# Feed-forward stages of a decoder trunk: six seven-product pairs per duo, and a running sum that ScalarE copies into the PSUM banks

## Chip, cores and metric

The kernel runs on one core of a Trainium2 chip. The metric is the time of one execution in microseconds (us), measured on the device; the kernel before took 2179.21 us (median of 3 runs, 2178.29 to 2180.29). One execution was also recorded by the hardware profiler; the profile and the trace are of that one.

## What is computed

A trunk of two layers on 256 tokens of width 2048, in float32: a gated linear attention mixer, a feed-forward layer, a differential attention mixer, a feed-forward layer. The change is in the two feed-forward layers:

```python
D_MODEL, SEQ, D_FF = 2048, 256, 5632

def swiglu(h, w_gate_up, w_down):
    gate, up = jnp.split(h @ w_gate_up, 2, axis=-1)
    return (jax.nn.silu(gate) * up) @ w_down

f = swiglu(rmsnorm(x, pre_ffn_g[i]), ffn_w_gate_up[i], ffn_w_down[i])
x = x + rmsnorm(f, post_ffn_g[i])
```

## The kernel before

**Matmuls in three products.** TensorE is given operands in a rounded float32 form. Each float32 operand is split in a high part (`hi`, the rounded value) and a low part (`lo`, what rounding left), and a product of two operands is three matmuls: high by high, high by low, low by high. `triple` (L438) issues these three for one stationary block of 128 tokens and 512 columns of weights; `mm_act` (L361) does so twice, for the two row blocks that one weight unit holds.

**Weights.** A weight unit is 128 x 1024 numbers, 512 KB. `weight_stream` lists all units in the order of use, `load` (L256) fetches them on SP's queue into five raw buffers, and `convert` splits them: ScalarE casts the high part (L294) and VectorE subtracts to get the low part (L296). `take` (L349) hands out the next unit and lets `pump` convert further ones; nine pairs of `hi` and `lo` buffers bound how far conversion may run ahead, and the five raw buffers how far loads may.

**Duos and pairs.** A gate chunk and an up chunk of 512 columns are computed together as a "duo" (`duo_apart`, L485), over eight pairs of row blocks. A plain pair takes 8 triples, 24 matmuls, and two weight units. A fast pair uses seven products in place of eight (a 2 x 2 block scheme): 7 triples, 21 matmuls. For that VectorE adds the two raw units in four ways (`sums`, L310, the adds at L317, 128 x 512 each), and four operands `a`, `b`, `c`, `d` are split, three of 128 x 1024 and one of 128 x 512 (`d`). The tokens' side of the seven products is formed once per stage by `build_forms` (L538). `FAST_FFN` names the fast pairs of the duos of chunks 2 to 10 (five pairs: 0, 2, 3, 4, 6), `FAST_SECOND` those of chunk 1 (four). Chunk 0 is computed without fast pairs.

**Banks.** PSUM has eight banks; six have the tag `acc`, two the tag `tp`. A duo uses all: products 0 to 5 in `acc`, product 6 and the last plain sum in `tp`. After the last fast pair, `early` (in `gated_duo`, L1120) takes products 0, 4, 5 and 6 out of their banks (a copy by ScalarE, L1137, and four VectorE operations, L1126); in the last plain pair `late` adds the remaining banks (L1126), ScalarE applies the SiLU (L1148) and VectorE multiplies gate by up (L1130). `gate_T` transposes the gated chunk on TensorE (`split_T`, L602) and splits it.

**The down product.** Its rows are taken in groups of one or two chunks (`FF_GROUPS`), each group in two halves of two output chunks (the group of one in a single call). `down_act` (L413) takes two banks per output chunk, one per 128 tokens, sums the products of the group there, and calls `evac`: the first group's sum is copied to the float32 tile `f` by ScalarE (L1200); every later group's is added to `f` by VectorE (L1202). With the last group `evac` also squares the sum (L630, ScalarE) and multiplies it by the gain (L1206, VectorE), and `add_norm` (L677) normalises and adds to `x`.

**Order.** `ffn_steps` alternates duos and down halves: duo, half, duo, half, with two duos and two halves per group of two chunks. The code is written in program order with small deferred steps (`defer`, `tick`); a scheduler then sets each engine's order from a simulated timeline and priorities. Each engine executes its queue in order.

## Time and profile before

| | |
|---|---|
| time, median of 3 runs | 2179.21 us |
| span of the profiled execution | 2177.2 us |
| time outside the span, against the median | 2.0 us |
| TensorE matmuls busy | 2162.6 us, 99% |
| TensorE weight loads busy | 1798.1 us, 83% |
| VectorE busy | 1932.7 us, 89% |
| ScalarE busy | 1267.2 us, 58% |
| granted TensorE clock, mean | 0.999 |
| first feed-forward stage | about 385 to 1062 us |
| second feed-forward stage | about 1500 to 2168 us |

The profiled execution has no separate time of its own outside the trace: its span stands for it, and 2.0 us are counted as lying around it. In the rows of a view, the first number of a timeline or chain row is the start in us from the span's start, the second the duration in us; a bracket tells how long the engine sat idle before the row and what ended that. In a row of groups the count stands behind x, then busy us and mean ns of one, then the idle time before them. In a row of waits stand the total, the times and the longest, in us. In a row of windows stand, after the length, busy us and instructions of TensorE, of its weight loads, of VectorE, ScalarE and GpSimd, then the granted clock, the DMA share and GB/s.

### The profile page before, as it was taken

Reading aid. Unit: us, or ns where it says so; the run is one execution under the profiler, and the core shown is the slowest. Engines: PE = TensorE matmul, PEld = TensorE weight load, DVE = VectorE, ACT = ScalarE, POOL = GpSimd, SP = SyncE. Lnnn points to the kernel's source line nnn. Section 1 sums busy time; section 2 is a strip of 40 time slices with the busy share of each in tenths; the row PEclk is TensorE's granted clock in tenths of the full one; section 3 lists DMA queues with packets and bytes.
Section 4 is the critical chain, followed back from the end, with each engine's and each line's share of the span. In section 5 each row is a group of like instructions: output and inputs, shape, how many; then the busy total and the mean of one; then the engine's idle time right before and its main releaser. Section 6 shows DMA issues by size and latency. Waiting matters only on the chain.

```text
span 2177.2 us, 28399 instructions
## 1 busy us (share of the span) xinstructions
PE 2162.6 (99%) x10098; PEld 1798.1 (83%) x10098; DVE 1932.7 (89%) x2646; ACT 1267.2 (58%) x1744; POOL 35.6 (2%) x66
## 2 busy tenths in 40 slices
PE   9999999999999999999999999999999999999998
PEld 8887788888888888888878888888888888888886
DVE  7989988998999999998898567889999999999986
ACT  8656665665655555554676455556566555555553
POOL 1000000000000000000000000000000000000000
PEclk9999999999999999999999999999999999999999
DMA  8545566666655566665757655465656555666664
GB/s 309 169 149 191 177 228 213 213 221 215 228 176 199 194 213 213 194 224 189 243 187 248 186 174 161 151 235 189 231 194 223 182 185 195 209 206 212 212 213 135
DMA packets 123315, 440.09 MB, mean 202 GB/s; under 512 B 13899, under 2 KB 16628, under 8 KB 121380
## 3 DMA queue, kind: packets, MB, share of 16 engines
q1 hardware_dynamic: 121996, 436.44, 60.2%
q10 hardware_dynamic: 1176, 1.84, 0.3%
q8 instruction: 79, 1.29, 0.2%
q14 instruction: 64, 0.52, 0.1%
HBM read 429.82 MB, written 9.97 MB: 202 GB/s over the span
## 4 chain that ended last, share of the span: by engine, by line
PE 96%; DVE 2%; DMA 1%; issue 1%; ACT 1%; POOL 0%; SPq 0%; DVEq 0%; POOLq 0%; ACTq 0%
PE acc L444 13%; PE acc L443 13%; PE acc L442 13%; PE acc L372 10%; PE acc L370 10%; PE acc L371 10%; PE acc L585 8%; PE acc L586 4%; PE tp L443 3%; PE tp L444 3%; PE tp L442 3%; PE tp L606 1%; DVE lo L296 1%; PE acc L1307 0%; PE acc L1346 0%
## 5 line engine op out<-in xcount | busy, mean ns | idle before, releaser
L294 ACT CAST hi<-raw 128x1024 fp32r<-128x1024 f32 x905 | 929.5, 1051 | 656.6 <-DVE raw L317 272.7
L296 DVE TENSOR_TENSOR lo<-raw,hi 128x1024 fp32r<-128x1024 f32 x903 | 1077.6, 1220 | 151.8 <-ACT hi L294 148.9
L370 PE MATMUL acc<-hi,f_ffn_gT 128*128 128x512 f32 x704 | 274.1, 390 | 0.0
L371 PE MATMUL acc<-lo,f_ffn_gT 128*128 128x512 f32 x704 | 274.0, 390 | 0.0
L372 PE MATMUL acc<-hi,f_ffn_gT 128*128 128x512 f32 x704 | 268.9, 389 | 0.0
L444 PE MATMUL acc<-hi,h_ffn 128*128 128x512 f32 x666 | 259.6, 390 | 0.0
L443 PE MATMUL acc<-lo,h_ffn 128*128 128x512 f32 x666 | 259.2, 389 | 0.0
L442 PE MATMUL acc<-hi,h_ffn 128*128 128x512 f32 x666 | 258.4, 390 | 0.0
L372 PEld LDWEIGHTS acc<-hi,f_ffn_gT 128*128 128x128 f32 x704 | 132.2, 188 | 27.3
L370 PEld LDWEIGHTS acc<-hi,f_ffn_gT 128*128 128x128 f32 x704 | 132.2, 188 | 27.2
L371 PEld LDWEIGHTS acc<-lo,f_ffn_gT 128*128 128x128 f32 x704 | 132.2, 188 | 27.0
L444 PEld LDWEIGHTS acc<-hi,h_ffn 128*128 128x128 f32 x666 | 125.0, 188 | 26.5 <-issue 0.6
L443 PEld LDWEIGHTS acc<-lo,h_ffn 128*128 128x128 f32 x666 | 125.1, 188 | 25.9
L442 PEld LDWEIGHTS acc<-hi,h_ffn 128*128 128x128 f32 x666 | 125.0, 188 | 25.9
L585 PE MATMUL acc<-h_q,hi 128*128 128x512 f32 x256 | 92.5, 401 | 0.0
L585 PE MATMUL acc<-h_kv,hi 128*128 128x512 f32 x256 | 90.6, 399 | 0.0
L585 PE MATMUL acc<-h_mix,hi 128*128 128x512 f32 x256 | 90.5, 398 | 0.0
L317 DVE TENSOR_TENSOR raw<-sum,raw 128x512 f32<-128x512 f32 x122 | 84.2, 690 | 3.5
L317 DVE TENSOR_TENSOR raw<-raw 128x512 f32<-128x512 f32 x122 | 84.2, 690 | 3.3
L317 DVE TENSOR_TENSOR raw<-raw,raw 128x512 f32<-128x512 f32 x122 | 83.9, 687 | 2.0
L317 DVE TENSOR_TENSOR sum<-raw,raw 128x512 f32<-128x512 f32 x122 | 83.5, 684 | 0.0
L586 PE MATMUL acc<-h_q,lo 128*128 128x256 f32 x256 | 73.2, 286 | 0.0
(416 smaller groups left out, 3912.4 us busy)
## 6 DMA issues: line engine op xcount, KB each, us to landing
raw<-in_w_gu_dram SPq DMA_DIRECT2D x352, 512.0 KB, 4.4
raw<-in_w_d_dram SPq DMA_DIRECT2D x176, 512.0 KB, 5.2
raw<-in_gla_w_r_dram SPq DMA_DIRECT2D x32, 512.0 KB, 4.4
raw<-in_gla_w_v_dram SPq DMA_DIRECT2D x32, 512.0 KB, 4.0
raw<-in_gla_w_out_dram SPq DMA_DIRECT2D x32, 512.0 KB, 4.5
raw<-in_w_v_dram SPq DMA_DIRECT2D x32, 512.0 KB, 4.7
raw<-in_w_k_dram SPq DMA_DIRECT2D x32, 512.0 KB, 4.0
raw<-in_diff_w_q_dram SPq DMA_DIRECT2D x32, 512.0 KB, 3.5
```

Of the source, the lines that this page charges most:

```text
L294: nc.scalar.copy(hi, src)
L296: eng.tensor_tensor(out=lo, in0=src, in1=hi.bitcast(F32), op=ALU.subtract)
L317: nc.vector.tensor_tensor(out=out, in0=in0, in1=in1, op=ALU.add)
L370: nc.tensor.matmul(ps, ah, rh, start=(kt == 0), stop=False)
L371: nc.tensor.matmul(ps, ah, rl, start=False, stop=False)
L372: nc.tensor.matmul(ps, al, rh, start=False, stop=(kt == 2 * ns - 1))
L442: nc.tensor.matmul(ps, ah, wh, start=first, stop=False)
L443: nc.tensor.matmul(ps, ah, wl, start=False, stop=False)
L444: nc.tensor.matmul(ps, al, wh, start=False, stop=last)
L585: nc.tensor.matmul(ps, lh, aT.both(kt), start=(kt == 0), stop=False)
L586: nc.tensor.matmul(ps[:, SEQ:], ll, aT.hi(kt), start=False, stop=(kt == KT - 1))
L606: nc.tensor.transpose(tp[:, j, :], src[:, j * P : (j + 1) * P], self.ident)
```

## The change

The change does five things in the feed-forward stages; lines of the changed kernel stand 2 to 27 lines further down.

1. `FAST_FFN` gets pair 5: six fast pairs in each of the nine duos of chunks 2 to 10, in both stages. The weights' stream follows by itself: four operands from the two units of that pair in place of two plain units. One more form step is built per stage.
2. The running sum no longer leaves PSUM by an addition. When `down_act` takes the banks of an output chunk of a later group, ScalarE copies the sum so far from `f` into them (40 copies per stage), the matmuls accumulate onto it (no start flag, `onto`), and `evac` is a copy back to `f` by ScalarE, or, with the last group, square and gain straight from the bank. VectorE's 40 adds per stage go.
3. `behind` adds order edges: the operations of `early` and `late` are queued, on their engine, behind the high and low part of the last unit converted so far among those up to the third after the last one taken. The numbers for the down product and the gate are 0: no edges.
4. The short operands `d` get two buffers of their own and two places in the tile of forms, in place of three places.
5. The side work (the bias table for the next mixer: small loads, four small VectorE steps, one matmul, a store) is deferred by 5 ticks in place of 20.

```diff
-FAST_FFN = (0, 2, 3, 4, 6)
+FAST_FFN = (0, 2, 3, 4, 5, 6)
+EARLY_BEHIND, LATE_BEHIND, DOWN_BEHIND, GATE_BEHIND = 3, 3, 0, 0
...
     def split(self, src, gp=False):
-        nc.scalar.copy(hi, src)
+        cast = nc.scalar.copy(hi, src)
...
-        eng.tensor_tensor(out=lo, in0=src, in1=hi.bitcast(F32), op=ALU.subtract)
+        rest = eng.tensor_tensor(out=lo, in0=src, in1=hi.bitcast(F32), op=ALU.subtract)
+        if not gp:
+            self.parts[self.n_conv] = cast.ins, rest.ins
...
+    @contextmanager
+    def behind(self, ahead):
+
+        made = [n for n in self.parts if n < self.n_take + ahead]
+        if not made or not ahead:
+            yield
+            return
+        cast, rest = self.parts[max(made)]
+        with self.tc.issue_after(cast), self.tc.issue_after(rest):
+            yield
...
-            nc.tensor.matmul(ps, ah, rh, start=(kt == 0), stop=False)
+            nc.tensor.matmul(ps, ah, rh, start=(kt == 0 and not onto), stop=False, skip_group_check=onto)
...
     def down_act(...):
                 ps[c] = [self.acc(), self.acc()]
+                if base:
+                    for i in range(2):
+                        self.nc.scalar.copy(ps[c][i], base(c, i))
...
     def duo_apart(...):
-                            late(bank, ps)
+                            with self.behind(LATE_BEHIND):
+                                late(bank, ps)
...
-                early(ps)
+                with self.behind(EARLY_BEHIND):
+                    early(ps)
...
     def ffn(...):
-        self.narrow, self.n_narrow = (fp, 0, 3), 0
+        self.narrow, self.n_narrow = (fp, 2, 2), 0
...
         def evac(grp, c, b, ps):
-            fc = f[0][:, b, c * C : (c + 1) * C]
-            if grp == first:
+            fc = part(c, b)
+            if grp != last:
                 nc.scalar.copy(fc, ps)
                 return
-            nc.vector.tensor_tensor(out=fc, in0=ps, in1=fc, op=ALU.add)
-            if grp == last:
-                self.square(fc, ss[b][:, c : c + 1])
-                fg = self.scratch() if c == 3 else fc
-                nc.vector.tensor_tensor(out=fg, in0=fc, in1=gains[c], op=ALU.mult)
...
+            self.square(ps, ss[b][:, c : c + 1])
+            nc.vector.tensor_tensor(out=fc, in0=ps, in1=gains[c], op=ALU.mult)
...
-                    self.defer(20, side)
+                    self.defer(5, side)
...
+            base = None if which == first else part
```

The order of VectorE's queue at the end of a duo in the second stage (chunk 7), where the last plain pair and the next down half are converted. Before: `lo` rows are low parts of 128 x 1024 (the first belongs to the last fast pair, the next two to the last plain pair, the others to the down half), L1126 are the bank operations.

```order
L296 TENSOR_TENSOR lo_16417<-raw_16295,hi_16416 128x1024
L296 TENSOR_TENSOR lo_16437<-raw_16355,hi_16436 128x1024
L296 TENSOR_TENSOR lo_16449<-raw_16372,hi_16448 128x1024
L296 TENSOR_TENSOR lo_16458<-raw_16384,hi_16457 128x1024
L296 TENSOR_TENSOR lo_16476<-raw_16411,hi_16475 128x1024
L296 TENSOR_TENSOR lo_16494<-raw_16420,hi_16493 128x1024
L296 TENSOR_TENSOR lo_16506<-raw_16440,hi_16505 128x1024
L296 TENSOR_TENSOR lo_16518<-raw_16452,hi_16517 128x1024
L1126 TENSOR_TENSOR hs_16545<-acc_16287,sg_16544 128x512
L296 TENSOR_TENSOR lo_16530<-raw_16461,hi_16529 128x1024
L1126 TENSOR_TENSOR sg_16544<-tp_16256,hs_16545 128x512
L1126 TENSOR_TENSOR sg_16544<-acc_16250,sg_16544 128x512
```

The same place in the changed kernel, where the bank operations are at L1148 and the low parts at L298.

```order
L298 TENSOR_TENSOR lo_16694<-raw_16547,hi_16693 128x1024
L298 TENSOR_TENSOR lo_16713<-raw_16607,hi_16712 128x1024
L298 TENSOR_TENSOR lo_16725<-raw_16639,hi_16724 128x1024
L298 TENSOR_TENSOR lo_16737<-raw_16651,hi_16736 128x1024
L1148 TENSOR_TENSOR hs_16809<-acc_16539,sg_16808 128x512
L298 TENSOR_TENSOR lo_16749<-raw_16685,hi_16748 128x1024
L1148 TENSOR_TENSOR sg_16808<-tp_16508,hs_16809 128x512
L298 TENSOR_TENSOR lo_16758<-raw_16697,hi_16757 128x1024
L1148 TENSOR_TENSOR sg_16808<-acc_16500,sg_16808 128x512
L298 TENSOR_TENSOR lo_16770<-raw_16716,hi_16769 128x1024
L1148 TENSOR_TENSOR hs_16810<-acc_16520,sg_16808 128x512
L1148 TENSOR_TENSOR hs_16809<-acc_16520,hs_16809 128x512
```

The first bank operation has moved from behind eight low parts to behind four, and the following ones alternate with low parts.

The order of ScalarE's queue in the changed kernel around a first half (output chunks 0 and 1) of a down product in the second stage: L296 are the casts of high parts, L1159 and L1170 the copy and the SiLU of the duo just ended, L438 the copies of the running sum `f_ffn` into banks, `acc_16320` and `acc_16321` for output chunk 0, `acc_16379` and `acc_16380` for output chunk 1.

```order
L1159 COPY sg_16270<-acc_15945 128x512
L296 CAST hi_16210<-raw_16149 128x1024
L438 COPY acc_16320<-f_ffn_14181 128x512
L296 CAST hi_16219<-raw_16161 128x1024
L438 COPY acc_16321<-f_ffn_14181 128x512
L296 CAST hi_16231<-raw_16178 128x1024
L296 CAST hi_16243<-raw_16190 128x1024
L296 CAST hi_16255<-raw_16202 128x1024
L1170 ACTIVATE sg_16270<-sg_16270,rs_ffn_0_13487 128x512
L438 COPY acc_16379<-f_ffn_14181 128x512
L296 CAST hi_16264<-raw_16214 128x1024
L438 COPY acc_16380<-f_ffn_14181 128x512
```

Before, this place held casts with the duo's copy and SiLU alone; the four copies into banks are new, between the casts of the half's units. `hi_16210`, `hi_16219` and `hi_16231` are its second to fourth unit, `hi_16255` its sixth, `hi_16264` its seventh. Output chunk 0 starts with the first unit and output chunk 1 with the third, so the copy for chunk 1 stands behind the cast of a unit that is used three units later.

More of the change, by code (lines that the diff above doesn't have):

```diff
@@ L1 @@
 import math
-from contextlib import ExitStack
+from contextlib import ExitStack, contextmanager
 import numpy as np
@@ L205, in __init__ @@
         self.subs = {}
+        self.parts = {}
         self.raws = {}
@@ L359, in free, with mm_act @@
         self.pump()
-    def mm_act(self, ps, aT, b, s, wp, ns):
+    def mm_act(self, ps, aT, b, s, wp, ns, onto=False):
         nc = self.nc
@@ L369, in mm_act @@
             rl = wlo[:, j * C : (j + 1) * C]
-            nc.tensor.matmul(ps, ah, rh, start=(kt == 0), stop=False)
-            nc.tensor.matmul(ps, ah, rl, start=False, stop=False)
-            nc.tensor.matmul(ps, al, rh, start=False, stop=(kt == 2 * ns - 1))
+            nc.tensor.matmul(ps, ah, rh, start=(kt == 0 and not onto), stop=False, skip_group_check=onto)
+            nc.tensor.matmul(ps, ah, rl, start=False, stop=False, skip_group_check=onto)
+            nc.tensor.matmul(ps, al, rh, start=False, stop=(kt == 2 * ns - 1), skip_group_check=onto)
     def chunk_act(self, aT, w, n, ns, evac, s0=0, head=0, tail=0, hook=None):
@@ L411, in chunk_act, with down_act @@
         evac(1, ps[1])
-    def down_act(self, aT, w, s0, order, ns, evac, skew=0):
+    def down_act(self, aT, w, s0, order, ns, evac, skew=0, base=None):
         ps, taken = {}, {}
@@ L420, in run @@
                 ps[c] = [self.acc(), self.acc()]
+                if base:
+                    for i in range(2):
+                        self.nc.scalar.copy(ps[c][i], base(c, i))
             if not b:
                 taken[u] = self.take(w, (c, s0 + s))
-            self.mm_act(ps[c][b], aT, b, s, taken[u], ns)
+            self.mm_act(ps[c][b], aT, b, s, taken[u], ns, base is not None)
             if s == ns - 1:
@@ L505, in duo_apart @@
                         if s == 7:
-                            late(bank, ps)
+                            with self.behind(LATE_BEHIND):
+                                late(bank, ps)
                         self.tick()
@@ L523, in duo_apart @@
             if last:
-                early(ps)
+                with self.behind(EARLY_BEHIND):
+                    early(ps)
     def rest_of(self, forms, i, name):
@@ L1174, in gate_T @@
             for b in range(2):
-                self.split_T(gTs[grp], 4 * grp.index(c), sg[:, b, :], b)
+                with self.behind(GATE_BEHIND):
+                    self.split_T(gTs[grp], 4 * grp.index(c), sg[:, b, :], b)
         def new_sg():
@@ L1197, in evac, with part @@
         def evac(grp, c, b, ps):
-            fc = f[0][:, b, c * C : (c + 1) * C]
-            if grp == first:
+            fc = part(c, b)
+            if grp != last:
                 nc.scalar.copy(fc, ps)
                 return
-            nc.vector.tensor_tensor(out=fc, in0=ps, in1=fc, op=ALU.add)
-            if grp == last:
-                self.square(fc, ss[b][:, c : c + 1])
-                fg = self.scratch() if c == 3 else fc
-                nc.vector.tensor_tensor(out=fg, in0=fc, in1=gains[c], op=ALU.mult)
-                if c == 3:
-                    fgs = [f[0][:, b, i * C : (i + 1) * C] for i in range(3)] + [fg]
-                    after(b, self.add_norm(fgs, b, ss[b]))
+            self.square(ps, ss[b][:, c : c + 1])
+            nc.vector.tensor_tensor(out=fc, in0=ps, in1=gains[c], op=ALU.mult)
+            if c == 3:
+                after(b, self.add_norm([part(i, b) for i in range(4)], b, ss[b]))
+        def part(c, b):
+            return f[0][:, b, c * C : (c + 1) * C]
         f = []
@@ L1235, in done @@
             def done(c, b, ps, grp=which):
-                (self.urgent(evac) if skew else evac)(grp, c, b, ps)
-            self.down_act(gTs[which], wd, 2 * which[0], down_order(which, chunks), 2 * len(which), done, skew)
+                if skew:
+                    self.urgent(evac)(grp, c, b, ps)
+                else:
+                    with self.behind(DOWN_BEHIND):
+                        evac(grp, c, b, ps)
+            base = None if which == first else part
+            self.down_act(gTs[which], wd, 2 * which[0], down_order(which, chunks), 2 * len(which), done, skew, base)
     def values(self, vp, aT, rs, i, steps, every):
```

## The prediction

> **What bounds the kernel now.** I read the page first, then the windows of the feed-forward stage, then VectorE's own waits there. The span line, the busy line and the chain that ended last, by engine:
>
> ```profile
> span 2177.2 us, 28399 instructions
> PE 2162.6 (99%) x10098; PEld 1798.1 (83%) x10098; DVE 1932.7 (89%) x2646; ACT 1267.2 (58%) x1744; POOL 35.6 (2%) x66
> PE 96%; DVE 2%; DMA 1%; issue 1%; ACT 1%; POOL 0%; SPq 0%; DVEq 0%; POOLq 0%; ACTq 0%
> ```
>
> The end is set by matmuls following matmuls: 96% of the chain is TensorE, and VectorE is close behind with 89%. The span is 2177.2 us and the median of the three runs 2179.2, so about 2 us lie around the span; I keep those 2 us and subtract from the median.
>
> All of the change lies in the two feed-forward stages, which repeat one period: two duos (a gate and an up chunk each), the two halves of a group's down product, two transposed gates. Three such periods from the view of windows, and two rows of the chain in order of time that mark the ends of the first:
>
> ```profile
> core 0: us, PE busy (x) PEld busy (x) DVE busy (x) ACT busy (x) POOL busy (x), PEclk, DMA share, GB/s
> 811.65:937.20 125.55, 125.55 (x564) 104.15 (x563) 118.45 (x141) 69.64 (x78) 0.00 (x0) 1.00 0.61 201
> 560.55:686.10 125.55, 125.55 (x565) 104.15 (x563) 118.96 (x141) 70.09 (x79) 0.00 (x0) 1.00 0.60 201
> 1690.00:1815.50 125.50, 125.50 (x564) 104.10 (x563) 118.83 (x142) 69.66 (x78) 0.00 (x0) 1.00 0.61 201
> 811.65 0.87 PE tp L606 x8
> 937.19 0.87 PE tp L606 x8
> ```
>
> A period takes 125.55 us in either stage, TensorE has no gap in it, at a granted clock of 1.00. It holds, by the code, 2 x (5x21 + 3x24) = 354 matmuls of duos and 16x12 = 192 of the down product, 546 of 512 columns, and 16 transposes (two groups of 0.87 us). So one matmul costs (125.55 - 1.74) / 546 = 0.2267 us. VectorE is idle for 125.55 - 118.45 = 7.1 us of the period. What that idle time is, from the view of waits of VectorE and from the groups of its instructions, both of the period 811.65 to 937.20:
>
> ```profile
> DVE lo L296 <- ACT hi L294: 5.5, 7, 1.6
> DVE f_ffn L1202 <- PE acc L372: 0.5, 1, 0.5
> DVE hs L1126 <- PE acc L444: 0.2, 1, 0.2
> L1202 DVE TENSOR_TENSOR f_ffn<-acc,f_ffn 128x512 f32<-128x512 f32 x8 | 5.5, 684 | 0.5 <-PE acc L372 0.5
> ```
>
> 6.2 us are real waits and 0.9 us small gaps between operations that depend on each other. So the stage is bound by TensorE, with VectorE 6.2 us per period from taking its place. That distance decides the case.
>
> **The change part by part.** *Six pairs for five.* A seven-product pair takes 21 matmuls, a plain one 24. Nine duos per stage change (chunk 1 keeps four pairs), 18 in all: 54 matmuls go, 54 x 0.2267 = 12.2 us, 1.36 us per period. Nothing else is in line with them, so all of it comes off the end if TensorE stays fed.
>
> *What the sixth pair costs VectorE.* Its timeline gives the price back to back:
>
> ```profile
> 724.42 0.68 DVE L1126 TENSOR_TENSOR hs<-acc,sg 128x512 f32<-128x512 f32 x1
> 725.02 0.68 DVE L1126 TENSOR_TENSOR hs<-acc,hs 128x512 f32<-128x512 f32 x1
> 725.62 1.22 DVE L296 TENSOR_TENSOR lo<-raw,hi 128x1024 fp32r<-128x1024 f32 x1
> ...
> 813.94 0.68 DVE L317 TENSOR_TENSOR raw<-raw,raw 128x512 f32<-128x512 f32 x1
> ...
> 820.73 0.69 DVE L317 TENSOR_TENSOR raw<-raw,raw 128x512 f32<-128x512 f32 x1
> ...
> 834.20 5.76 DVE L296 TENSOR_TENSOR lo<-raw,hi 128x1024 fp32r<-128x1024 f32 x5
> 841.17 1.23 DVE L296 TENSOR_TENSOR lo<-raw,hi 128x1024 fp32r<-128x1024 f32 x1 [1.22 <-ACT hi L294]
> 843.38 2.36 DVE L296 TENSOR_TENSOR lo<-raw,hi 128x1024 fp32r<-128x1024 f32 x2 [0.98 <-ACT hi L294]
> ```
>
> Starts, not durations, count, since neighbours overlap: an operation of 512 columns takes 0.60 us (724.42 to 725.02), a low part (5.76 - 1.22) / 4 = 1.135, a whole pair (four sums, four low parts) 820.73 - 813.94 = 6.79. A pair for a plain one, whose two low parts take 2.27, is + 4.52 us; two per period, + 9.04.
>
> *What the running sum gives back.* The eight adds of a period (L1202, row above) leave VectorE: 8 x 0.60 = - 4.8 us, with the 0.5 us that the first of them waits. Net VectorE work: + 4.24 us per period, while the period shrinks by 1.36. Of 7.1 us idle 1.5 are left, 1.0 of it the small gaps: **0.5 us of waits per period are free**. If w us of waits remain, the period is 124.19 + (w - 0.5), with nine periods (18 duos) in the kernel. w up to 0.5 gives the full 12.2; w = 1.86 gives nothing; each further 0.1 costs 0.9 us.
>
> *Which waits remain.* Those of today sit in one place, the head of each down half: after five low parts in a row the next cast lacks its weights. ScalarE's timeline there:
>
> ```profile
> 837.38 1.06 ACT L294 CAST hi<-raw 128x1024 fp32r<-128x1024 f32 x1 [0.64 <-DMA raw<-in_w_d_dram]
> 840.09 1.05 ACT L294 CAST hi<-raw 128x1024 fp32r<-128x1024 f32 x1 [1.65 <-DMA raw<-in_w_d_dram]
> 845.97 1.05 ACT L294 CAST hi<-raw 128x1024 fp32r<-128x1024 f32 x1 [1.57 <-DMA raw<-in_w_d_dram]
> ```
>
> There are five raw buffers, and a load starts when a low part frees one, so a fast run of low parts always outruns the loads. In the changed order (VectorE's rows in the part on the change) the bank operations no longer come after eight low parts in a row but after four, and then alternate with them: three operations of 0.60, 1.8 us, lie ahead of the low parts that wait today for 1.22 and 0.98, 2.2 us. About 0.4 us per half is left, w = 0.8 per period: 0.3 over what is free, nine times, 2.7 us. The ends: w = 0 (VectorE starts each stage ahead, and its lead is eaten first), and 5.7, all of today's but the add's 0.5. I take 0.8 since the row it comes from is the same place.
>
> *ScalarE.* It gets eight copies into banks and eight out of them per period, and 2 x 1.67 us of casts (three long and a short one for two long). The price of a copy out of a bank, and of a short cast, and how long such a copy sat waiting:
>
> ```profile
> L1200 ACT COPY f_ffn<-acc x16: 571/587/589, 492.8 to 1643.7; 128x512 f32<-128x512 f32 x16
> L294 ACT CAST f_ffn_rest<-sum 128x512 fp32r<-128x512 f32 x98 | 60.3, 615 | 20.8 <-DVE sum L317 20.8
> ACT f_ffn L1200 <- PE acc L372: 12.9, 10, 4.8
> ```
>
> A copy into a bank has no row; I take 0.59 as for one out of it, and 0.6 either way would not matter: 69.6 + 16 x 0.59 + 3.3 = 82.4 us of 124.2, 66%. What matters is the queue. A copy out that waits for a matmul holds the casts behind it, and so VectorE: up to 4.8 us once, by the third row. Such a wait needs VectorE well ahead, and takes only from its lead; I count it into w's upper end.
>
> *Edges at early and late.* They put a bank operation behind the conversion of the third unit taken ahead. Queued behind it are the following low parts; who waits for it is the down product, whose first banks (by the built program's allocation) are those of products 0 and 5, the first two that early releases, and 24 matmuls of the last plain pair, 5.4 us, lie between. *One more form step per stage* (6 operations, under 3 us) falls beside the first chunk, where 16 low parts, 18 us, face 192 matmuls, 43 us: nothing. *The side work* (the bias table of the next mixer) moves from tick 20 to tick 5 with its small loads and one store on SP's queue, and the store waits for a copy by VectorE with weight loads queued behind it:
>
> ```profile
> 534.31 0.33 SPq L259 DMA_DIRECT2D raw<-in_w_gu_dram  x1
> 534.76 0.29 SPq L761 DMA_DIRECT2D bias_vec<-hs  x1
> 536.49 32.61 SPq L259 DMA_DIRECT2D raw<-in_w_gu_dram  x10
> ```
>
> Today the next load comes 1.7 us after the store (534.76 to 536.49) and no matmul waits; five raw buffers cover it earlier too, and uncovered it is those 1.7 us, once. *The fourth narrow home* for the short products costs nothing: one buffer more can only free a cast earlier.
>
> *The end.* The last add goes; square and gain now read the bank. The timeline's last steps, and a row of waits for the same pattern in the output projections, where gain and square already read one bank:
>
> ```profile
> 2168.51 0.69 DVE L1202 TENSOR_TENSOR f_ffn<-acc,f_ffn 128x512 f32<-128x512 f32 x1 [2.95 <-PE acc L372]
> 2169.24 0.69 DVE L1206 TENSOR_TENSOR hs<-f_ffn,gain 128x512 f32<-128x512 f32 x1
> 2169.29 0.63 ACT L630 ACTIVATE junk<-f_ffn 128x512 f32<-128x512 f32 x1 [4.71 <-DVE f_ffn L1202]
> 2170.05 0.21 DVE L621 TENSOR_SCALAR st<-st,st 128x1 f32<-128x1 f32 x1
> ACT junk L630 <- DVE f_mix L1066: 18.2, 4, 8.6
> ```
>
> Today add, then square beside gain: 1.54 us from 2168.51 to 2170.05. In the projections ScalarE waits for VectorE although both only read, so I count square then gain, 0.63 + 0.69 and two hops of 0.09 (2169.20 to 2169.29): 1.5 us, no gain. The Trainium skill ("PSUM — Partial Sum Buffer", PSUM bank collisions raise a hardware error) says that two engines on one bank and quadrant are kept apart, reads against reads included; the last row agrees. Side by side, which the rule forbids, 0.7 us would be saved: 2169.0 for 2169.7.
>
> The sum: 2179.2 - 12.2 + 2.7 = **2169.7 us**.
>
> **The rivals.** *VectorE becomes the bound (slower).* Place: the head of the down halves and the five pairs in a row (2 to 6) ahead of it, where VectorE loses 6.79 - 21 x 0.2267 = 2.0 us per pair on TensorE. If 2.4 of today's 5.7 us of waits stay, the period is 126.1 and the kernel 2184; with all of them 129.4 and 2214. It decides from w = 1.86. For it: the waits come from loads (three rows of ScalarE) that no edit makes faster, and 16 new copies per period stand between the casts. Against it: they stand behind runs of five low parts that the new order breaks up. The Trainium skill ("Perfetto Trace Analysis", Identifying the Most-Contended Engine) says that matmul busy time misleads and that the engine with the highest occupancy is the one to relieve, weight loads counting for TensorE; by that, VectorE (118.45 of 125.55, 94%) is ahead of TensorE (104.15, 83%) and must not be loaded. The chain speaks against the rule here, as the matmuls follow without a gap.
>
> *Something between.* w of 1.3 to 2.4: 2175 to 2184, no change that can be told.
>
> *The copies into banks are in line (no change, at worst slower).* ScalarE's rows in the part on the change show where: in a first half, output chunk 1 starts with the third unit, but the copy for its first bank stands behind the cast of the sixth, which waits for its load. TensorE waits if that cast is less than three units, 3 x 12 x 0.2267 = 8.2 us, ahead of it. Place: the eight first halves of six-pair groups, four per stage; price: up to the wait of one load, 1.65 us (row 840.09), and a copy with its hop, 0.68, for each: 19 us, 2188, if every one loses it all, some 7 us, 2176, if a third is lost. Against it: eight low parts and eight bank operations, 14 us, stand between the end of the fast pairs and the last unit, while TensorE needs 5.4 + 21.8 us for the same.
>
> *The change does not do what it says.* No: the order holds 54 matmuls fewer, 40 VectorE operations more and 182 of ScalarE more.
>
> **How the numbers follow.** Forecast with w from 0 to 1.2: 2167 to 2174, chance 0.62. Between (0.14) or copies in line in part (0.09): 0.23. VectorE bound (0.12) or all copies in line (0.03): 0.15. A measurement here tells 0.2% (4.4 us) from no change: faster is below 2174.8, slower above 2183.6. The range leaves out the slower cases and 0.05 below (1.2 us from the end of the first stage, whose adds go too): 2165.5 to 2181.
>
> **What would show it.** In the changed profile the period between gate transposes should be 124.2 to 124.6, VectorE 98 to 99% busy in it, no add behind the down product, waits of VectorE under 1.5 us per period. TensorE rows waiting for low parts show the slower rival; TensorE waiting for ScalarE's copies (L438) the third. I am wrong if the period is above 125.2, or if TensorE has no gap and the time still doesn't fall.

## The result, and the profile after

The changed kernel takes 2186.86 us (median of 6 runs, 2184.46 to 2189.43), the kernel before 2179.02 us (6 runs, 2178.29 to 2180.29): a ratio of 1.0034, with a 95% interval of 1.0024 to 1.0044. It is slower by 7.8 us, where 9.5 us less was forecast. The profiled execution took 2185.24 us.

The page of the changed kernel: span, busy time of each engine, and the chain that ended last.

```profile
span 2183.3 us, 28530 instructions
PE 2159.4 (99%) x10044; PEld 1787.7 (82%) x10044; DVE 1964.0 (90%) x2686; ACT 1356.9 (62%) x1926; POOL 36.3 (2%) x66
PE 82%; DVE 13%; issue 2%; DMA 1%; ACT 1%; SPq 0%; POOL 0%; DVEq 0%; POOLq 0%; ACTq 0%
```

The 54 matmuls are gone, and the span is 6.1 us longer. In the chain VectorE went from 2% to 13%. Three periods of the first stage, one after the other, in the view of windows (columns as in the prediction), and VectorE's waits, first of 684.10 to 809.65, then of a period of the second stage, 1648.97 to 1773.69:

```profile
559.38:684.10 124.72, 124.48 (x557) 103.05 (x556) 121.54 (x143) 78.65 (x98) 0.00 (x0) 1.00 0.61 202
684.10:809.65 125.55, 125.07 (x557) 102.90 (x556) 122.05 (x144) 79.46 (x98) 0.00 (x0) 1.00 0.62 201
809.65:937.27 127.62, 125.40 (x557) 102.73 (x556) 122.15 (x144) 79.09 (x98) 0.00 (x0) 1.00 0.62 198
```

```profile
DVE f_ffn_gT L631 <- ACT f_ffn_gT L630: 2.1, 1, 2.1
DVE lo L298 <- ACT hi L296: 0.2, 1, 0.2
```

```profile
DVE lo L298 <- ACT hi L296: 2.4, 3, 1.7
```

VectorE works 121.5 to 122.2 us of a period (118.45 before) and still waits 2.3 to 2.4 us in the first two, 3.2 us in the third. The loss grows over these periods: against the floor of 124.19 the three periods lose 0.5, 1.4 and 3.4 us, and the third of the second stage, 127.01 us, loses 2.8.

In the first of these lists the wait at the head of the down halves is almost gone, 0.2 us where it was 5.5; but a new one has come, VectorE's half of the split of a transposed gate (L631), which waits for ScalarE's half (L630). Of the 2.4 us in the second list 1.65 lie at 1649.37 us, right behind a gate's transposes too. TensorE sees it from the other side. Its waits in the first stage, 438 to 1054 us:

```profile
PE acc L385 <- ACT f_ffn_gT L630: 2.3, 3, 1.8
PE tp L461 <- DVE lo L298: 1.0, 4, 0.2
```

The first line counts stops of the down product for a gate, the second stops inside the duos for a low part, the sign that the prediction gave for its slower rival. TensorE's timeline at the longest of them, in the third period:

```profile
860.38 0.62 PE L460 MATMUL acc<-hi,h_ffn 128*128 128x512 f32 x2
...
862.11 1.09 PE L628 MATMUL tp<-ident,sg 128*128 128x128 f32 x8
865.04 0.49 PE L385 MATMUL acc<-hi,f_ffn_gT 128*128 128x512 f32 x1 [1.84 <-ACT f_ffn_gT L630]
```

VectorE's and ScalarE's timelines of the same microseconds:

```profile
857.24 3.49 DVE L298 TENSOR_TENSOR lo<-raw,hi 128x1024 fp32r<-128x1024 f32 x3
860.64 1.41 DVE L1152 SCALAR_TENSOR_TENSOR sg<-hs,rs_ffn,sg 128x512 f32<-128x512 f32 x2
```

```profile
863.45 1.04 ACT L296 CAST hi<-raw 128x1024 fp32r<-128x1024 f32 x1 [4.91 <-DVE raw L321]
864.40 1.07 ACT L630 CAST f_ffn_gT<-tp 128x512 fp32r<-128x512 f32 x2
```

Read them as one chain: the gate's multiplication (L1152) stands behind three low parts and ends at 862.05; the transposes start 0.06 us later; ScalarE is held by a cast that waited 4.91 us for a sum of VectorE; the down product stands for 1.84 us. In the kernel before, the built order had matmuls of the down product and of the next duo (L442) behind the transposes, and they filled that round trip. TensorE's timeline of the kernel before at the same place:

```profile
861.34 1.03 PE L606 MATMUL tp<-ident,sg 128*128 128x128 f32 x8
862.13 0.48 PE L370 MATMUL acc<-hi,f_ffn_gT 128*128 128x512 f32 x1
...
862.91 0.39 PE L442 MATMUL acc<-hi,h_ffn 128*128 128x512 f32 x1
```

The end of the first stage, VectorE's timeline and then TensorE's; `h_kv` is the normalised input of the mixer that follows:

```profile
1079.06 0.69 DVE L1226 TENSOR_TENSOR f_ffn<-acc,gain 128x512 f32<-128x512 f32 x1 [4.48 <-DMA gain<-in_post_ffn_g_dram]
...
1084.76 3.49 DVE L298 TENSOR_TENSOR lo<-raw,hi 128x1024 fp32r<-128x1024 f32 x3
...
1091.09 0.35 DVE L669 SCALAR_TENSOR_TENSOR h_kv<-tp,gcols,h_kv 128x128 fp32r<-128x128 f32 x1
```

```profile
1087.32 0.50 PE L385 MATMUL acc<-hi,h_kv 128*128 128x512 f32 x1 [1.17 <-ACT h_kv L667]
1087.66 0.39 PE L386 MATMUL acc<-lo,h_kv 128*128 128x512 f32 x1
1091.50 0.79 PE L387 MATMUL acc<-hi,h_kv 128*128 128x512 f32 x1 [3.44 <-DVE h_kv L669]
1092.09 0.63 PE L385 MATMUL acc<-hi,h_kv 128*128 128x512 f32 x1
1092.52 0.63 PE L386 MATMUL acc<-lo,h_kv 128*128 128x512 f32 x1
```

TensorE waits 1.17 and 3.44 us for parts of that input, first for ScalarE's half, then for VectorE's, which stands behind low parts. Then its matmuls follow each other at 0.43 us, not 0.23.

The account, from the starts of TensorE's matmuls in both traces (all that a start lies more than 0.08 us beyond the usual 0.2267): inside the two stages 6.0 and 5.8 us more than before, at the end of the first 4.7, at the end of the second 1.0, together 17.5; less 12.2 for the 54 matmuls leaves 5.3 of the 6.1 us. The other 0.8 us I can't assign.

### The profile page after: what moved, and what is told of

The parts are those of the page before. It is cut to its first block, busy times and chain, and to the rows that moved or that the text cites. A ratio compares the mean times of both kernels' runs of the same rounds, so it can differ in the third digit from the quotient of the medians.

```text
span 2183.3 us, 28530 instructions
## 1 busy us (share of the span) xinstructions
PE 2159.4 (99%) x10044; PEld 1787.7 (82%) x10044; DVE 1964.0 (90%) x2686; ACT 1356.9 (62%) x1926; POOL 36.3 (2%) x66
## 3 DMA queue, kind: packets, MB, share of 16 engines
q10 hardware_dynamic: 1176, 1.84, 0.2%
## 4 chain that ended last, share of the span: by engine, by line
PE 82%; DVE 13%; issue 2%; DMA 1%; ACT 1%; SPq 0%; POOL 0%; DVEq 0%; POOLq 0%; ACTq 0%
PE acc L385 10%; PE acc L387 10%; PE acc L386 10%; PE acc L461 10%; PE acc L462 10%; PE acc L460 10%; PE acc L607 8%; DVE lo L298 7%; PE acc L608 4%; DVE raw L321 3%; PE tp L461 2%; PE tp L462 2%; PE tp L460 2%; DMA raw<-in_w_d_dram 1%; DVE sum L321 1%
## 5 line engine op out<-in xcount | busy, mean ns | idle before, releaser
L296 ACT CAST hi<-raw 128x1024 fp32r<-128x1024 f32 x923 | 944.2, 1051 | 527.1 <-DVE raw L321 197.1
L298 DVE TENSOR_TENSOR lo<-raw,hi 128x1024 fp32r<-128x1024 f32 x921 | 1095.8, 1219 | 111.2 <-ACT hi L296 109.2
L461 PE MATMUL acc<-lo,h_ffn 128*128 128x512 f32 x612 | 238.3, 389 | 0.0
L462 PE MATMUL acc<-hi,h_ffn 128*128 128x512 f32 x612 | 238.2, 389 | 0.0
L460 PE MATMUL acc<-hi,h_ffn 128*128 128x512 f32 x612 | 227.0, 390 | 0.0
L460 PEld LDWEIGHTS acc<-hi,h_ffn 128*128 128x128 f32 x612 | 114.9, 188 | 23.8
L462 PEld LDWEIGHTS acc<-hi,h_ffn 128*128 128x128 f32 x612 | 114.9, 188 | 23.7
L321 DVE TENSOR_TENSOR raw<-raw 128x512 f32<-128x512 f32 x140 | 96.7, 691 | 4.2
L321 DVE TENSOR_TENSOR raw<-sum,raw 128x512 f32<-128x512 f32 x140 | 96.5, 690 | 3.9
L321 DVE TENSOR_TENSOR raw<-raw,raw 128x512 f32<-128x512 f32 x140 | 96.4, 689 | 3.2
L321 DVE TENSOR_TENSOR sum<-raw,raw 128x512 f32<-128x512 f32 x140 | 95.7, 684 | 0.0
L1223 ACT COPY f_ffn<-acc 128x512 f32<-128x512 f32 x80 | 46.7, 586 | 77.5 <-PE acc L387 77.5
```

The source lines that it names most:

```text
L296: cast = nc.scalar.copy(hi, src)
L298: rest = eng.tensor_tensor(out=lo, in0=src, in1=hi.bitcast(F32), op=ALU.subtract)
L321: nc.vector.tensor_tensor(out=out, in0=in0, in1=in1, op=ALU.add)
L460: nc.tensor.matmul(ps, ah, wh, start=first, stop=False)
L461: nc.tensor.matmul(ps, ah, wl, start=False, stop=False)
L462: nc.tensor.matmul(ps, al, wh, start=False, stop=last)
```

## The experiments

The theory, called V below: VectorE has become the bound. Its work and its waits together no longer fit into TensorE's 124.2 us, and the gaps in the stages, the late gates among them, come from its lateness. The rivals: the order edges hold the gate back (E), or ScalarE's copies into banks stand in line (C).

| run | what differs | us, median (range) | ratio to before, 95% interval |
|---|---|---|---|
| changed kernel | | 2186.86 (2184.46 to 2189.43) | 1.0024 to 1.0044 |
| 1 | five pairs | 2178.54 (2178.28 to 2179.36) | 0.9987 to 1.0005 |
| 2 | before, six pairs | 2220.86 (2220.14 to 2222.0) | 1.0177 to 1.0205 |
| 3 | no edges | 2214.59 (2214.17 to 2216.29) | 1.0151 to 1.0179 |
| 4 | three sums at half width | 2169.09 (2167.61 to 2171.65) | 0.9943 to 0.9968 |
| 5 | third gain buffer | 2186.28 (2184.56 to 2187.81) | 1.0018 to 1.0041 |
| 6 | 4 low parts per period on GpSimd | 2167.27 (2166.58 to 2167.88) | 0.9928 to 0.9955 |
| 7 | fast pairs three and three | 2182.27 (2179.01 to 2184.78) | 1.0001 to 1.0019 |
| 8 | 5 and 6 together | 2166.95 (2166.18 to 2167.74) | 0.9928 to 0.9953 |
| 9 | 2 low parts per period on GpSimd | 2174.82 (2173.23 to 2176.74) | 0.9969 to 0.9987 |
| 10 | 6 without edges | 2177.14 (2176.18 to 2182.02) | 0.9985 to 1.0003 |
| 11 | seven pairs, 16 low parts on GpSimd | 2303.59 (2302.65 to 2305.01) | 1.0554 to 1.0583 |
| 12 | 6 with the adds on VectorE | 2204.35 (2203.31 to 2205.47) | 1.0098 to 1.0132 |

**1. The sixth pair taken back.**

```diff
-FAST_FFN = (0, 2, 3, 4, 5, 6)
+FAST_FFN = (0, 2, 3, 4, 6)
```

> The changed kernel with the five pairs of before (54 matmuls more), all else of the change kept. Theory V (VectorE is the bound: the sixth pair takes its slack, and all TensorE gaps in the stages follow from its lateness): VectorE has 118.45 - 4.8 = 113.7 us of work for 125.55 us, no TensorE waits for low parts or gates in the stages, period 125.55 as before; only the end of the first stage may keep its + 2.7 us: 2177 to 2182. Theory E (the order edges hold the bank operations back, so the gate comes late): the gate stalls, some 2.5 us per stage, and the end of the first stage stay: 2183 to 2187. Theory C (ScalarE's copies into the banks are in line): also 2183 to 2187, with TensorE waiting for them or for casts behind them.

A period of it in the view of windows:

```profile
686.22:811.77 125.55, 125.55 (x564) 104.13 (x562) 114.47 (x132) 77.63 (x95) 0.00 (x0) 1.00 0.61 201
```

2178.54 us, the time of before, with no gap in the period and VectorE at 114.5 us. The edges and the copies into banks are all there, so neither makes TensorE wait by itself: E and C fall for five pairs. For six pairs run 3 decides on E, and run 6, which keeps edges and copies, on C.

**2. The sixth pair alone**, on the kernel before.

```diff
-FAST_FFN = (0, 2, 3, 4, 6)
+FAST_FFN = (0, 2, 3, 4, 5, 6)
...
-        self.narrow, self.n_narrow = (fp, 0, 3), 0
+        self.narrow, self.n_narrow = (fp, 2, 2), 0
```

> The kernel before with the sixth pair alone (and the buffers for its short operands, without which it finds no room): VectorE keeps its adds, no copies into banks, no edges. Theory V: VectorE's work per period is 118.45 + 9.04 = 127.5 us, above TensorE's 124.2, and at least 1 us of small gaps stays: period 128.5 to 130, nine periods + 27 to + 40 us, 2206 to 2219. Theories E and C: neither edges nor copies are there, so the full gain of the sixth pair shows: 2167 to 2170.

```profile
688.02:817.84 129.82, 126.40 (x557) 102.56 (x556) 127.13 (x153) 71.71 (x82) 0.00 (x0) 1.00 0.60 196
```

2220.86 us, 2 us above V's range. VectorE works 127.13 of 129.82 us, as the bookkeeping of V had it (127.5): here it plainly sets the period.

**3. Without the edges.**

```diff
-EARLY_BEHIND, LATE_BEHIND, DOWN_BEHIND, GATE_BEHIND = 3, 3, 0, 0
+EARLY_BEHIND, LATE_BEHIND, DOWN_BEHIND, GATE_BEHIND = 0, 0, 0, 0
```

> The changed kernel without the order edges at early and late. Theory E: the bank operations and with them the gates come earlier, TensorE no longer waits for gates; at least the 2.5 us per stage come back: 2178 to 2182, and 2170 to 2175 if the late low parts in the duos came from the edges too. Theory V: VectorE has the same work, only in another order: 2184 to 2192. Theory C: as the changed kernel, 2185 to 2189.

2214.59 us: E forecast a faster kernel, and V 2184 to 2192. Both were wrong: it is 27.7 us above the changed kernel, with the same instructions on VectorE. The place is the end of the fast pairs. ScalarE, VectorE and TensorE there:

```profile
589.26 0.58 ACT L1159 COPY sg<-acc 128x512 f32<-128x512 f32 x1 [5.51 <-PE acc L462]
589.87 0.59 ACT L438 COPY acc<-f_ffn 128x512 f32<-128x512 f32 x1
590.40 1.04 ACT L296 CAST hi<-raw 128x1024 fp32r<-128x1024 f32 x1
```

```profile
591.47 1.23 DVE L298 TENSOR_TENSOR lo<-raw,hi 128x1024 fp32r<-128x1024 f32 x1 [3.23 <-ACT hi L296]
```

```profile
591.49 0.50 PE L460 MATMUL tp<-hi,f_ffn_rest 128*128 128x512 f32 x1 [1.82 <-ACT hi L296]
```

Without edges ScalarE's copy out of a bank stands ahead of a cast and waits 5.51 us for its last matmul; behind the copy the cast waits, behind the cast VectorE for 3.23 us, and behind both TensorE. The edges put that copy behind the casts. So the edges save waits; that is what lets six pairs come within 8 us of the kernel before.

**4. Lighter sums.** In the feed-forward stages three of the four sums of a fast pair leave out half their columns, so part of the product is missing.

```diff
+        h = C // 2 if self.narrow[1:] == (2, 2) else C
-        add(r1[:, :C], r1[:, :C], r2[:, :C])
-        add(r2[:, :C], r2[:, :C], r2[:, C:])
+        add(r1[:, :h], r1[:, :h], r2[:, :h])
+        add(r2[:, :h], r2[:, :h], r2[:, C : C + h])
         add(t2, r1[:, :C], r2[:, C:])
-        add(r1[:, C:], t2, r1[:, C:])
+        add(r1[:, C : C + h], t2[:, :h], r1[:, C : C + h])
```

> The changed kernel with three of the four sums of each fast pair in the feed-forward stages done on half their columns (the other half is left out, so part of the product is wrong): VectorE loses up to 3 x 0.3 us per pair, some 10 us per period, the order of dependences stays. Theory V: TensorE has no gap in the stages, period 124.2, VectorE waits about 10 us per period: 2167 to 2172 (the upper end if the end of the first stage keeps its 2.7 us). Theories E and C: edges, copies and ScalarE's work are the same, so most of the gaps stay: 2181 to 2189.

```profile
685.43:809.64 124.21, 124.21 (x558) 103.07 (x557) 113.87 (x144) 79.89 (x99) 0.00 (x0) 1.00 0.61 203
```

2169.09 us: the period is the forecast's 124.2, and nothing but VectorE's work was changed in the program's text. V holds. One thing is not separated: the scheduler works with the durations it expects, and with lighter sums it also put matmuls of the next duo behind the gate's transposes again.

**5. A buffer of its own for the third gain**, whose load VectorE was seen to wait 4.48 us for.

```diff
-        g = self.hs.tile([P, C], F32, tag="gain", name=self.uid("gain"), bufs=2)
+        g = (pool or self.hs).tile([P, C], F32, tag="gain", name=self.uid("gain"), bufs=1 if pool else 2)
...
-                    gains[c] = self.gain(post, c)
+                    gains[c] = self.gain(post, c, fp if c == 2 else None)
```

> The changed kernel with a buffer of its own for the gain of output chunk 2 in the last group. In the changed kernel's trace VectorE waits 4.5 us for a gain's load at the end of the first stage (the load starts when a multiplication frees one of two buffers), and the norm that the next chunk needs is queued behind that wait. Theory G (this wait makes TensorE's 1.2 and 3.4 us of waits there and the low clock after them): they go, 2.7 to 5 us less, 2182 to 2184.5; the end of the second stage, where the same wait exists, may give another 1 us. Theory Q (the low parts queued ahead of the norm make it late, the load only fills a time in which VectorE had nothing to do): 2185.5 to 2188.

VectorE's and TensorE's rows at the end of the first stage:

```profile
1081.01 0.69 DVE L1226 TENSOR_TENSOR f_ffn<-acc,gain 128x512 f32<-128x512 f32 x1 [3.81 <-ACT junk L652]
```

```profile
1093.41 0.80 PE L387 MATMUL acc<-hi,h_kv 128*128 128x512 f32 x1 [2.73 <-DVE h_kv L669]
```

2186.28 us, no change. The wait for the load became a wait of 3.81 us for ScalarE's square, which reads the same bank first; TensorE still waits 1.17 us and then 2.73 us (3.44 in the changed kernel). My theory G falls: the releaser that a view names is the last of several, and here, by the difference of the two waits, the one before it had come only about 0.7 us earlier (4.48 - 3.81). Low parts queued ahead of the norm stay the likeliest reason, argued from the rows above and not tested by itself.

**6. Low parts on GpSimd.** The second and sixth unit of each down half (four per period) are subtracted by GpSimd.

```diff
         self.pool_lo.update((3, 5))
+        self.pool_lo.update(pool_units(self.stream))
...
+def pool_units(stream):
...
+        if name[:3] == "w_d":
+            seen[name] = seen.get(name, -1) + 1
+            if seen[name] % 8 in (1, 5):
+                out.append(n)
...
```

> The changed kernel with the low parts of the second and sixth unit of each half of a down product on GpSimd, 4 per period. Theory V (VectorE's total work and its waits set the stages): VectorE loses 4 x 1.135 = 4.5 us per period, more than the 1.4 us that TensorE lacks, period 124.2 to 124.4, all 13 us of the stages' gaps go; with 2 to 3 us left at the end of the first stage 2169 to 2174. Theory P (GpSimd and VectorE hold each other up when both work, or a low part of 2.4 us instead of 1.2 comes too late itself): TensorE waits for GpSimd's low parts or VectorE's operations get longer; 2180 to 2195.

A period, GpSimd's group in the whole run, and one low part of VectorE beside one of GpSimd (726.73 to 729.14):

```profile
683.78:807.97 124.19, 124.19 (x558) 103.01 (x556) 119.51 (x140) 79.19 (x99) 9.90 (x4) 1.00 0.61 203
```

```profile
L309 POOL TENSOR_TENSOR lo<-raw,hi 128x1024 fp32r<-128x1024 f32 x46 | 116.7, 2536 | 1209.4 <-ACT hi L307 1133.1 <-PE acc L473 51.8 <-DVE sg L1159 14.0
```

```profile
726.73 2.41 POOL L309 TENSOR_TENSOR lo<-raw,hi 128x1024 fp32r<-128x1024 f32 x1 [5.57 <-ACT hi L307]
```

```profile
728.27 1.96 DVE L309 TENSOR_TENSOR lo<-raw,hi 128x1024 fp32r<-128x1024 f32 x1
```

2167.27 us, 10 to 16 us below the kernel before by the interval: the full computation, at 124.19 per period. V holds, and this version beats both kernels. By its code the edit can also move an edge, since `behind` passes over units that GpSimd subtracts. Part of P is there too: the low part beside GpSimd's took 1.96 us instead of 1.22, and VectorE's busy time fell by 2.5 us in this period and by 3.8 and 2.9 in its neighbours, not by 4.5. The Trainium skill ("Perfetto Trace Analysis", Optimizing Scalar/DVE Operations) warns that work moved from VectorE to GpSimd might not help, since both share a read port of SBUF. Here a sixth to nearly half of it was lost, and the rest was enough.

**7. Three and three.** Plain pairs at 3 and 7.

```diff
-FAST_FFN = (0, 2, 3, 4, 5, 6)
+FAST_FFN = (0, 1, 2, 4, 5, 6)
```

> The changed kernel with the plain pairs at 3 and 7, so that no more than three fast pairs stand in a row (before: five). Theory L (the lead is lost in the five pairs in a row, 2.0 us of it per pair, and a plain pair between gives 5.44 - 2.27 = 3.2 us back): the waits for low parts inside the duos, some 3.3 us per stage, go, gate waits shrink: 2176 to 2181. Theory T (only the total of VectorE's work and waits per period counts): the same loss in other places, 2184 to 2189.

2182.27 us, between the two theories, 4.6 us below the changed kernel. The run of five pairs is part of the loss. Run 7 doesn't show what the rest is: it stands 15 us above run 6.

**8. GpSimd and the gain buffer**, the edits of 5 and 6 together.

> The changed kernel with both: four low parts of a period on GpSimd, and the gain buffer. Theories V and G: all that the change lost comes back, 2179.2 - 12.2 = 2167, and up to 1 us less if the end of the first stage is shorter than in the kernel before: 2165 to 2169.5. If only V holds, as with GpSimd alone, 2169 to 2174; if P holds, 2178 to 2193.

2166.95 us, which can't be told from run 6: as in run 5, the buffer gives nothing.

**9. Half of run 6**, one low part per half.

```diff
-            if seen[name] % 8 in (1, 5):
+            if seen[name] % 8 in (1,):
```

> The changed kernel with one low part per half of a down product on GpSimd, two per period (the run with four: VectorE 119.5 us busy in a period of 124.19, 2167.3 us). By that run a low part on GpSimd takes about 0.64 us net off VectorE, so two leave it some 120.8 us. Theory K (a knee: the loss starts where work, small gaps of 1.2 us and waits of 2.3 us exceed TensorE's 124.2): 120.8 + 3.5 = 124.3, at the knee, nearly the whole gain shows: 2167 to 2171. Theory D (each microsecond of VectorE's work costs the same, in a straight line): half way between 2186.9 and 2167.3, 2175 to 2179.

A period of it:

```profile
734.49:859.12 124.63, 124.48 (x558) 102.93 (x557) 119.80 (x143) 79.55 (x98) 4.98 (x2) 1.00 0.61 201
```

2174.82 us, just under D's range and 3.8 us above K's: there is no sharp knee. TensorE loses 0.44 us in this period although VectorE is idle for 4.8 us of it, and the gap lies among the pairs in a row, at a matmul that waits for a low part. So the sum over a period does not decide alone; it matters what comes late inside the pairs.

**10. Run 6 without edges**, with the edit of run 3.

> Four low parts per period on GpSimd, and no order edges at early and late (without GpSimd the edges' absence cost 27.7 us). Theory S (the edges only save waits of a VectorE that has no slack): with some 4.7 us of slack per period little is lost, 2167 to 2172. Theory E2 (without them the bank operations stand at the wrong place whatever the slack, and TensorE waits): 2180 to 2195.

2177.14 us: 9.9 us lost, where the lack of the edges cost 27.7 us without GpSimd. Neither theory's number; with the room that GpSimd gives, about two thirds of what the edges save is no longer needed.

**11. Seven pairs**, all sixteen low parts of the down units of a period on GpSimd, over run 6.

```diff
-FAST_FFN = (0, 2, 3, 4, 5, 6)
+FAST_FFN = (0, 1, 2, 3, 4, 5, 6)
...
-            if seen[name] % 8 in (1, 5):
+            if seen[name] % 8 in (0, 1, 2, 3, 4, 5, 6, 7):
...
-        self.narrow, self.n_narrow = (fp, 2, 2), 0
+        self.narrow, self.n_narrow = (fp, 2, 1), 0
```

> Seven fast pairs per duo (54 matmuls fewer again, - 12.2 us; the short products with two buffers and one place) with all sixteen low parts of the down units of a period on GpSimd. Theory K: VectorE 119.5 + 9.0 - 12 x 0.64 = 120.8 us of 122.8, 2.0 us below, less than the 3.5 us of gaps and waits: a period of 123 to 124.5, 2156 to 2170. If GpSimd's low parts of 2.5 us, eight in a row per half, come too late themselves or hold VectorE up more: over 2175.

TensorE's waits inside the seven pairs, two of them one pair apart, and VectorE's gate multiplications of 600 to 1000 us:

```profile
727.12 0.50 PE L471 MATMUL tp<-hi,f_ffn_rest 128*128 128x512 f32 x1 [1.17 <-ACT hi L307]
...
733.91 0.50 PE L471 MATMUL tp<-hi,f_ffn_rest 128*128 128x512 f32 x1 [1.16 <-ACT hi L307]
```

```profile
L1163 DVE SCALAR_TENSOR_TENSOR sg<-hs,rs_ffn,sg 128x512 f32<-128x512 f32 x12 | 22.8, 1902 | 8.2 <-ACT sg L1181 8.1
```

2303.59 us. In the pairs TensorE follows VectorE's beat, 733.91 - 727.12 = 6.79 us per pair in place of 21 x 0.2267 = 4.76. My reading, not tested by itself: VectorE can run ahead only by the nine ring buffers, so relief in the down halves does not carry through seven pairs. And the gate multiplications, all of which lie beside a low part of GpSimd here, take 1.90 us, where the same operation (L1152) took 0.7 in the changed kernel.

**12. The running sum back on VectorE**, over run 6; `evac` is that of the kernel before.

```diff
-            if grp != last:
+            if grp == first:
                 nc.scalar.copy(fc, ps)
                 return
+            nc.vector.tensor_tensor(out=fc, in0=ps, in1=fc, op=ALU.add)
...
-            base = None if which == first else part
+            base = None
```

> Four low parts per period on GpSimd, six pairs and edges as in the run of 2167.3 us, but the running sum as in the kernel before: eight adds per period on VectorE, no copies into banks. Theory V: VectorE 119.5 + 8 x 0.60 = 124.3 us, with small gaps of 1.2 us a period of at least 125.5, with 2.3 us of waits up to 127.8: nine periods, + 12 to + 32 us, 2179 to 2200. Theory R (the room that GpSimd and the edges give is enough, the running sum needn't leave VectorE): 2167 to 2172.

A period of it:

```profile
738.56:865.75 127.19, 125.70 (x557) 102.61 (x556) 123.29 (x149) 71.43 (x82) 10.56 (x4) 1.00 0.62 197
```

2204.35 us, above V's range and 37 us above run 6. So the copies into banks are worth having once six pairs are in; what the change lacked was a little more room on VectorE.

In order of VectorE's work in the periods shown, kernels with six pairs and edges line up: 119.51 us (run 6) 2167, 119.80 (run 9) 2175, 122.05 (changed kernel) 2187, 123.29 (run 12) 2204. The 113.87 us of run 4 gain nothing over run 6, since TensorE has no gap in the period of either.

Run 12 also bears on the order behind the gates. TensorE's timeline at the transposes in this period:

```profile
738.56 1.03 PE L639 MATMUL tp<-ident,sg 128*128 128x128 f32 x8
739.35 0.48 PE L472 MATMUL acc<-lo,h_ffn 128*128 128x512 f32 x1
```

Four matmuls of the next duo follow the transposes at this place of the period in runs 6, 9, 10 and 12 alike; in the changed kernel none does. Their times are 2167, 2175, 2177 and 2204 us. So that order alone does not give run 6 its time.

## Why the prediction was wrong, point by point

- **54 matmuls, 12.2 us, a floor of 124.19 per period: right.** Runs 4 and 6 stand at 124.21 and 124.19.
- **VectorE's net work, + 4.24 us per period: right within a microsecond.** 122.69 was worked out, 121.54, 122.05 and 122.15 were measured. Run 2 (127.13 for 127.5) bears out the sixth pair's price.
- **"Which waits remain", w = 0.8: the step that failed.** w stands for VectorE's waits in a period. The waits measured are 2.3 to 2.4 us, 3.2 in the third period, and the small gaps 1.2 us for 1.0 (125.55 - 122.05 - 2.3). The argument was right about the place that it looked at: at the head of the down halves the wait fell from 5.5 us to between 0.2 and 1.4, and 0.8 was forecast. But the new wait at the gates, some 2 us, is not in it. The forecast asked only how the waits of before would shrink, and not which work on VectorE now came late, and whose round trip through TensorE and ScalarE was then uncovered. With 2.3 the formula gives 126.0, less the 0.6 to 1.1 us by which the work was overpriced 124.9 to 125.4; the first two periods were 124.72 and 125.55. That alone is bookkeeping, since work, gaps and waits make up any period; that VectorE sets it is what runs 4, 6 and 12 show. And the formula has one period nine times over, while the third took 127.62 us: the forecast counted VectorE's lead at the start of a stage only as a reserve, and not what happens at the gates once it is used up.
- **The slower rival came true, with its pairs.** The five pairs in a row are where low parts come late (runs 7, 9, 11). Its price, 2184 with 2.4 us of waits, is near what came, but partly by luck: it put 17 us into the periods (9 x 1.9), where the stages lost 11.8 and the ends of the stages 5.7. Its chance, 0.12, was too small. The Trainium skill ("Perfetto Trace Analysis", Identifying the Most-Contended Engine), set aside because the matmuls followed without a gap, pointed at the engine that decided: the chain of before could not show how near the next bound was.
- **The edges at early and late, which have no term in the sum: they save 27.7 us here** (run 3). I priced what an edge delays and not the copy that without it waits ahead of the casts. It was the nearest row to that, a copy waiting 4.8 us with casts behind, that was put into an upper end and left there.
- **ScalarE: right.** 79.46 us busy (82.4 forecast), no matmul waits for L438, and the copy into a bank takes as long as the one out of it:

```profile
L438 ACT COPY acc<-f_ffn x80: 571/579/596, 594.0 to 2158.6; 128x512 f32<-128x512 f32 x80
```

- **The end of the first stage: wrong in direction.** It stood only as a possible gain of 1.2 us, at 0.05, and no loss was counted. 4.7 us are lost there, in the two waits and in the low clock after them.
- **The last steps of the kernel: right.** Square and multiplication follow each other; the 1.0 us of the account lie earlier, at a gate (2147 us):

```profile
2174.82 0.60 ACT L652 ACTIVATE junk<-acc 128x512 f32<-128x512 f32 x1 [4.75 <-PE acc L387]
```

```profile
2175.54 0.69 DVE L1226 TENSOR_TENSOR f_ffn<-acc,gain 128x512 f32<-128x512 f32 x1 [2.57 <-ACT junk L652]
```

What stays open: how much of the recovery in runs 4 and 6 is VectorE's lighter load and how much the scheduler's other order behind the gates, which comes with it. The changed kernel's stops right behind those transposes bound its direct share: 0.28, 0.28 and 1.88 us in the first stage, 0.28, 0.28 and 1.70 in the second, start to start beyond the usual, 4.7 of the 19.6 us between it and run 6. Open too is the last step at the end of the first stage. Lighter work on VectorE helps there, for in run 6 TensorE's two waits are 1.05 and 1.39 us, with no low clock behind them; but one of 2.27 us, with the low clock, is there in run 1 too, with five pairs.

## What to carry to other kernels

When a change spends the slack of the second-busiest engine, don't ask only whether its busy time fits: add the waits that it can't lose, and look for a round trip (VectorE to TensorE to ScalarE and back) that is hidden only because that engine was early. Runs 7, 9 and 11 suggest that an engine that may run ahead by a few buffers has to be balanced within each run of work as long as those buffers, not only over the period. And an instruction that waits for a far-off result must not stand ahead of casts that others need: the order edges that prevent it were worth more here (27.7 us) than the matmuls saved (12.2).

## What the hardware showed

**A short stop of TensorE can cost twice.** After the waits of 1.17 and 3.44 us quoted above, matmuls of 512 columns came every 0.43 us, and the granted clock of that window was 0.56. It happened in run 3 too, after a wait of 1.82 us. Windows of the changed kernel and of run 3:

```profile
1092.00:1096.00 4.00, 4.00 (x12) 3.03 (x11) 4.00 (x12) 2.38 (x5) 0.26 (x1) 0.56 1.03 413
```

```profile
593.50:597.50 4.00, 4.00 (x12) 3.12 (x12) 4.00 (x4) 3.31 (x4) 0.00 (x0) 0.58 0.83 242
```

Five to ten matmuls at half rate are 1 to 2 us more. The length of the stop does not decide it alone. Seven of the nine stops of 2.2 us, start to start, in run 3's stages were followed by it, and one of 1.82 us in run 12; none of the seven stops of 2.2 to 2.7 us in run 11's stages was, nor the one of 2.11 us in the changed kernel (865.04), nor any of the seventeen stops of 1.5 to 1.6 us in run 2's. The Trainium skill ("TensorE: Matmul & The Clock Gate", Part 1: The HAM clock gate) gives 426.7 ns for 512 columns at the low clock, and the traces agree (1092.52 - 1092.09 = 0.43); it names an idle window of about 3.4 us as what lowers the clock, and here a wait of 1.82 us, and in run 12 one of 1.43, was enough.

**GpSimd slows VectorE.** Besides the 1.96 and 1.90 us above, the 62 low parts of VectorE that overlap one of GpSimd's in run 6 took 1.57 us on average, the other 815 took 1.22. GpSimd's own low part took 2.54 us on average there, and 2.41 in run 11 where VectorE was idle beside it (18 of them): it takes twice as long as VectorE's even alone, and the overlap adds little on average.
